# Attention for 64 heads on one core: 18 groups of scores on VectorE instead of 16, and the order of all engines remade

## The chip, the core and the metric

The kernel runs on one core of one Trainium2 chip. A core has several engines that run side by side, each with its own list of instructions in a fixed order: TensorE (PE; its weight loads are listed as PEld) multiplies matrices and writes to PSUM, ScalarE (ACT) computes functions such as exp, VectorE (DVE) and GpSimd (POOL) do elementwise work, SyncE (SP) issues transfers, and 16 DMA engines carry these. An instruction waits on semaphores until what it needs is done; everything behind it on its engine waits with it. The metric is the time of one execution in device microseconds; lower is better.

## The reference

The inputs q, k and v have 8 batches, 8 heads, 512 positions and 64 dimensions each, in float32. The output has the same shape.

```
scores = einsum('bhqd,bhkd->bhqk', q, k) / sqrt(64)
scores = scores - scores.max(axis=-1, keepdims=True)
attn   = exp(scores)
attn   = attn / attn.sum(axis=-1, keepdims=True)
out    = einsum('bhqk,bhkd->bhqd', attn, v)
```

So there are 64 heads with 512 x 512 scores each, 16.8 million exponentials in all.

## The kernel before

**Tiling.** The 64 heads are worked off as 32 pairs (g from 0 to 31, h is 0 or 1). For each pair, q, k and v are loaded by SP (256 KB a transfer, line 509) and cast to fp16 by GpSimd (`cast`, lines 515 and 525). PE transposes q and k (line 558), and VectorE copies the result from PSUM into the tile `tqk` (line 571). PE then computes the scores with keys on the partitions (line 598), in blocks of 128 keys (c from 0 to 3) by 512 queries. Two blocks make a *group*: one PSUM tile `st` of 128 x 1024, of which there are three. There are 128 groups; the last is cut into two halves, so the code counts 129, numbered 0 to 128. Each pair but the first and the last takes four groups in the order c, h; in the last pair the first two groups (124, 125) belong to head 0 and the others to head 1.

**Two ways to an exponential.** Most groups go to ScalarE: one ACTIVATE of exp over 128 x 1024 (line 602) writes the fp16 tile `pt`. The groups listed in `ON_DVE` go to VectorE instead, as six instructions. `raise_` (line 625) reads the scores from PSUM and writes the bits of a power of two with a linear fraction, as a 16-bit integer, into the tile `pd`. That frees the PSUM tile. Then five passes over SBUF, `pass_`: L642 takes the mantissa, L651 the exponent (tile `pe`), L659 squares, L661 is a linear function, and L665 multiplies into `pd`. The exponential of such a group is the sum of `pe` and `pd`, and PE adds both: the product with v has two parts for each block of it instead of one.

**Values.** The weights are not divided before the product with v. The v tile has a column of ones, so that each product (line 704) gives the sum of the weights beside the 64 outputs. A *unit* is 128 queries of one head: four products, one for each c, and one more for each block that VectorE has raised. Seven units share one PSUM tile `o`. When a tile is full, VectorE takes the reciprocal of the sums (L671) and multiplies (L676) into a ring in SBUF, from which SP stores heads (lines 690 and 694). Two PSUM banks serve these tiles and the transposes in turn. The last head, (31, 1), has its own path: `last_values` (line 720), then `finish` (L733, L734) and its own store (L740). The last two other stores are issued by ScalarE.

**What sets the order.** Everything is written out in one list of steps, which the class `Plan` makes while the kernel is built. `Plan.run` steps through a clock of its own, 5 ns at a time, and keeps the time at which each engine comes free. Its methods choose for each engine what it does next: `step_pe` among scores, transposes and values; `step_dve` among copies, raises, reciprocals, multiplies and, when none of these is about to come, passes; `step_pool` and `trigger` place the casts (each waits for a certain VectorE instruction, because the two share access to SBUF in the plan's model); `step_sp` loads and stores. The constants at the head of the class are this model: durations of instructions, waiting times from engine to engine (`TO_ACT`, `TO_DVE`, `TO_PE`, `EXP_DONE`, `PASS_DONE`), rules for what is held back for what (`LATE_*`, `HURRY`, `SOON`, `BACKLOG`, `WAIT`, `SLACK`), and due times for casts (`PAIR`, `DUEK`, `DUEV`, `PRE`). The chip executes the order that comes out, with real waits on semaphores; the plan's clock is not part of the program. `KNOWN` lists groups whose exponential gets one more wait, on a cast six casts back. At most `BITS` = 2 raised groups may be unfinished at a time.

The choice between the engines is made in `scores`:

```
m, grp = self.m, self.groups[self.m]
on_dve = self.for_dve(m)          # m in ON_DVE
if on_dve:
    self.ready.append((t + self.TO_DVE, "raise", (m,)))
```

Of the kernel before, what the change touches and what calls it, by code (L numbers as in the profile page):

```python
# [13 lines left out]
EXP = mybir.ActivationFunctionType.Exp  # L14
# [2 lines left out]

class Plan:

    SLOT, EXP, EXP_DONE, EXP_FIXED = 216, 853, 181, 64  # L20
    INTO, OUT_OF = 96, 96
    TRANSPOSE, V_UNIT = 222, 128
    TO_ACT, TO_DVE, TO_PE = 220, 210, 60

    COPY, NORM, RAISE = (601, 690), (50, 133), (1132, 1215)
    RECIPROCAL = 115
    SCALE, PRODUCT, EXTRA = 333, 600, 29
    COPY_1 = (400, 190)
    NORM_COLUMN, PASS_DONE = 67, 115
    PASSES = (SCALE, SCALE, PRODUCT, SCALE, PRODUCT)  # L30
    BITS = 2
    NEEDS = (None, None, 0, 2, 3)
    FIRST_EXP = 5000
    STEP = 5
    CALM, KEEN = 9000, 4
    FIRST_UNIT = 4
    KNOWN, OVER = (13, 15, 18, 20, 22, 24, 27, 42, 50, 61, 69, 97), 6
    ON_DVE = (5, 10, 16, 25, 28, 39, 44, 54, 63, 66, 74, 81, 91, 96, 103, 116)

    LATE_NORM, LATE_COPY, HURRY, SOON, BACKLOG = 700, 1500, 800, 160, 600  # L40
    LATE_MUL, WAIT = 400, 200
    SLACK, AHEAD = 0, 2

    CAST, CAST_PORT, CAST_DONE, TO_POOL = 557, 475, 130, 150
    SCALE_PORT, PRODUCT_PORT, GAP, REACH = 271, 537, 20, 5
    FIRST_LAND, LOAD, STORE, LATENCY, ISSUE = 5200, 752, 376, 2300, 470
    QUEUED, URGENT = 3500, 16
    PAIRED, STORE_ISSUE = 18, 520
    RAW, QK16, NV, NU = 7, 5, 12, 112
    PAIR, DUEK, DUEV, DUEL, PRE = 3300, 3550, 6000, 5000, 0  # L50

    def __init__(self, groups, pairs, first):
        self.groups, self.pairs = groups, pairs
# [27 lines left out]

        late = {grp[0][0] for m, grp in enumerate(groups) if m in self.ON_DVE}
        due = []
# [121 lines left out]
    def for_dve(self, m):  # L205
        return m in self.ON_DVE

# [126 lines left out]
    def step_dve(self, t):  # L334
# [14 lines left out]
        if now:  # L349
# [15 lines left out]
            if kind == "rec":  # L365
                self.dve = t + self.RECIPROCAL
                self.ready.append((self.dve + self.PASS_DONE, "mul", what))
# [6 lines left out]
            elif kind == "finish":  # L374
                self.dve = t + self.RECIPROCAL + self.PASS_DONE + self.NORM[0] + 4 * self.NORM_COLUMN
            elif kind == "copy":
# [523 lines left out]
```

## Time and profile before

| what | us |
|---|---|
| three runs | 114.32, 114.25, 113.85 |
| median | 114.25 |
| span of the profiled execution, first to last instruction | 112.6 |
| ScalarE busy | 105.7 |
| PE busy | 103.9 |
| VectorE busy | 100.8 |
| GpSimd busy | 66.0 |

The profile gives the span of the execution it recorded, and no other time of it; the runs are timed around the span. Busy time counts overlapping instructions once. Consecutive instructions of VectorE or ScalarE overlap a little, so the price of one in a dense row is the distance from its start to the next start, which is less than its listed duration. L12 stands for line 12 of the kernel. A bracket [0.87 <-PE o L704] says how long the engine was idle before an instruction and what released it. The granted clock of TensorE is 0.999 of full speed over the span.

### The profile page before, as it was taken

The numbers are of one execution on the slowest core, as the hardware profiler recorded it, in microseconds if no ns is written. First come the engines' busy times: TensorE is split into PE (matmuls) and PEld (weight loads), VectorE is DVE, ScalarE is ACT, GpSimd is POOL, SyncE is SP. The second block draws the span as 40 slices with busy tenths as digits, with TensorE's granted clock in tenths as the row PEclk, the third lists the DMA queues.
The fourth block names the chain that finished last, engine by engine and source line by source line (L and its number), as shares of the span: only waits on it lengthen the run. The fifth ranks groups of instructions, "written<-read, shape, count | busy, mean of one in ns | idle before, by whom it ended". The sixth has DMA issues, their size and how long they took to land.

```text
span 112.6 us, 4414 instructions
## 1 busy us (share of the span) xinstructions
PE 103.9 (92%) x1731; PEld 69.8 (62%) x1731; DVE 100.8 (90%) x227; ACT 105.7 (94%) x118; POOL 66.0 (59%) x127
## 2 busy tenths in 40 slices
PE   7987979999799998999989999899999999999980
PEld 7744545766376675748656767577567577675660
DVE  1547999999999999999999999999999999998390
ACT  4688999999999999999999999999999999999970
POOL 2136778639854886496495786876784855600000
PEclk9999999999999999999999999999999999999999
DMA  3999999999999999999999999999998984143344
GB/s 97 269 319 359 346 349 349 354 336 348 348 348 347 350 332 342 348 357 349 372 363 381 353 350 377 345 377 370 332 368 285 357 286 144 53 142 99 121 139 163
DMA packets 35093, 33.84 MB, mean 301 GB/s; under 512 B 2304, under 2 KB 35072, under 8 KB 35072
## 3 DMA queue, kind: packets, MB, share of 16 engines
q1 hardware_dynamic: 34496, 33.04, 90.0%
q10 hardware_dynamic: 576, 0.52, 1.4%
q8 instruction: 13, 0.21, 0.9%
q14 instruction: 8, 0.07, 0.2%
HBM read 25.17 MB, written 8.39 MB: 298 GB/s over the span
## 4 chain that ended last, share of the span: by engine, by line
DMA 36%; PE 24%; DVE 14%; POOL 12%; issue 8%; SPq 2%; ACT 2%; POOLq 0%; ACTq 0%
DMA q<-in_q_dram 21%; PE o L704 12%; DMA out_dram<-ring 9%; PE st L598 8%; POOL qkp L525 8%; DMA v<-in_v_dram 6%; POOL vp L515 3%; DVE pd L625 3%; DVE ring L676 3%; PE tp L558 2%; DVE tqk L571 2%; ACT pt L602 2%; SPq L509 2%; DVE pd L665 1%; DVE m L659 1%
## 5 line engine op out<-in xcount | busy, mean ns | idle before, releaser
L602 ACT ACTIVATE pt<-st 128x1024 f16<-128x1024 f32 (+1 forms) x110 | 100.2, 1136 | 0.4 <-PE st L598 0.4
L704 PEld LDWEIGHTS <-pt 128*128 128x128 f16 x880 | 38.8, 98 | 12.1 <-issue 10.2
L704 PE MATMUL o<-vp,pt 128*128 128x65 f16 x880 | 45.3, 194 | 0.4 <-POOL vp L515 0.3
L598 PE MATMUL st<-tqk 64*128 64x512 f16 (+1 forms) x250 | 41.7, 380 | 2.6 <-ACT pt L602 1.3
L525 POOL CAST qkp<-k 128x512 f16<-128x512 f32 x31 | 22.2, 717 | 11.7 <-DVE rc L671 5.0
L525 POOL CAST qkp<-q 128x512 f16<-128x512 f32 x30 | 21.8, 725 | 9.0 <-DVE rc L671 5.3
L515 POOL CAST vp<-v 128x512 f16<-128x512 f32 x32 | 21.4, 679 | 9.2 <-PE st L598 3.6
L676 DVE TENSOR_TENSOR ring<-o,rc 128x448 f32<-128x448 f32 (+2 forms) x37 | 22.2, 602 | 0.4
L704 PE MATMUL o<-vp,pe 128*128 128x65 f16 x128 | 21.8, 194 | 0.0
L704 PE MATMUL o<-vp,pd 128*128 128x65 f16 x128 | 21.7, 192 | 0.0
L558 PE MATMUL tp<-ident,qkp 128*128 128x128 f16 x248 | 19.6, 220 | 1.4 <-DVE tqk L571 0.8
L558 PEld LDWEIGHTS <-qkp 128*128 128x128 f16 x248 | 14.4, 97 | 9.8 <-issue 4.9
L571 DVE COPY tqk<-tp 128x1024 f16<-128x1024 f16 x30 | 20.2, 680 | 0.0
L625 DVE TENSOR_SCALAR pd<-st 128x1024 uint16<-128x1024 f32 x16 | 19.4, 1214 | 0.7 <-PE st L598 0.7
L598 PEld LDWEIGHTS <-tqk 64*128 64x128 f16 x250 | 10.6, 93 | 11.7 <-issue 4.6
L704 PEld LDWEIGHTS <-pe 128*128 128x128 f16 x128 | 12.5, 98 | 3.5 <-issue 3.4
L704 PEld LDWEIGHTS <-pd 128*128 128x128 f16 x128 | 12.5, 98 | 0.0
L665 DVE TENSOR_TENSOR pd<-pd,m 128x1024 f16<-128x1024 f16 x16 | 10.9, 682 | 0.0
L659 DVE TENSOR_TENSOR m<-m 128x1024 f16<-128x1024 f16 x16 | 10.9, 680 | 0.0
L671 DVE RECIPROCAL rc<-o 128x7 f32<-128x7 f32 (+2 forms) x37 | 7.2, 195 | 2.5 <-PE o L704 2.4
L661 DVE TENSOR_SCALAR m<-m 128x1024 f16<-128x1024 f16 x16 | 6.7, 416 | 0.1
L651 DVE TENSOR_SCALAR pe<-pd 128x1024 uint16<-128x1024 uint16 x16 | 6.5, 407 | 0.0
(52 smaller groups left out, 36.8 us busy)
## 6 DMA issues: line engine op xcount, KB each, us to landing
v<-in_v_dram SPq DMA_DIRECT2D x32, 256.0 KB, 5.9
k<-in_k_dram SPq DMA_DIRECT2D x31, 256.0 KB, 5.9
q<-in_q_dram SPq DMA_DIRECT2D x31, 256.0 KB, 5.9
out_dram<-ring SPq DMA_DIRECT2D x18, 256.0 KB, 5.4
out_dram<-ring SPq DMA_DIRECT2D x25, 128.0 KB, 2.9
k<-in_k_dram ACTq DMA_DIRECT2D x2, 128.0 KB, 2.7
q<-in_q_dram SPq DMA_DIRECT2D x2, 128.0 KB, 2.5
out_dram<-ring ACTq DMA_DIRECT2D x2, 128.0 KB, 1.9
```

The lines of the kernel that those rows point to most:

```text
L515: return nc.gpsimd.tensor_copy(out=vps[g % NV][:, :, :, 0:D], in_=raw[g]["v"][:, :, :, :])
L525: return nc.gpsimd.tensor_copy(out=dst, in_=src[:, :, :, :])
L558: reads[g] = nc.tensor.transpose(tps[g][:, n, i, :], qkp[g][:, n, i, :], ident)
L571: nc.vector.tensor_copy(out=tqk[g][:, :, :], in_=tps.pop(g).rearrange("p n i c -> p n (i c)"))
L598: nc.tensor.matmul(st[:, x, cols], kc, qc[:, cols], start=True, stop=True)
L602: ins = nc.scalar.activation(out=pt[:, :, cols], in_=st[:, :, cols], func=EXP, scale=scale, bias=SHIFT)
L625: nc.vector.tensor_scalar(out=r["pd"][:, :, :], in0=r["st"][:, :, :], scalar1=BITS, scalar2=BIAS, op0=AluOp.mult, op1=AluOp.add,)
L659: ins = nc.vector.tensor_tensor(out=m16, in0=m16, in1=m16, op=AluOp.mult)
L665: ins = nc.vector.tensor_tensor(out=u16, in0=u16, in1=m16, op=AluOp.mult)
L671: dve(nc.vector.reciprocal(out=rcs[u][:, 0:n], in_=o[:, x : x + n, D : D + 1]))
L676: nc.vector.tensor_tensor(out=ring[:, u % NU : u % NU + n, :], in0=o[:, x : x + n, 0:D], in1=rcs.pop(u)[:, 0:n].broadcast_to([P, n, D]), o ...
L704: nc.tensor.matmul(os[u // 7][:, u % 7, :], part[:, y * P : (y + 1) * P], vps[g % NV][:, h, c, :], start=(n == 0), stop=(n == len(parts) - 1),
```

## The change

The two kernels differ only in constants of `Plan`; all functions are the same, and their line numbers too. `ON_DVE` gets two more entries, 120 and 124, and nine of the sixteen others move by one to three. The waiting times and priorities of the model change, so that the plan comes out with another order on every engine.

```
-    SLOT, EXP, EXP_DONE, EXP_FIXED = 216, 853, 181, 64
-    INTO, OUT_OF = 96, 96
+    SLOT, EXP, EXP_DONE, EXP_FIXED = 216, 853, 201, 56
+    INTO, OUT_OF = 92, 88
-    TO_ACT, TO_DVE, TO_PE = 220, 210, 60
+    TO_ACT, TO_DVE, TO_PE = 260, 230, 60
-    RECIPROCAL = 115
+    RECIPROCAL = 125
-    NORM_COLUMN, PASS_DONE = 67, 115
+    NORM_COLUMN, PASS_DONE = 67, 125
-    CALM, KEEN = 9000, 4
+    CALM, KEEN = 11500, 4
-    ON_DVE = (5, 10, 16, 25, 28, 39, 44, 54, 63, 66, 74, 81, 91, 96, 103, 116)
+    ON_DVE = (5, 10, 15, 25, 29, 37, 46, 52, 63, 67, 75, 81, 88, 96, 101, 116, 120, 124)
-    LATE_NORM, LATE_COPY, HURRY, SOON, BACKLOG = 700, 1500, 800, 160, 600
-    LATE_MUL, WAIT = 400, 200
-    SLACK, AHEAD = 0, 2
-    CAST, CAST_PORT, CAST_DONE, TO_POOL = 557, 475, 130, 150
+    LATE_NORM, LATE_COPY, HURRY, SOON, BACKLOG = 1100, 600, 800, 260, 400
+    LATE_MUL, WAIT = 1350, 100
+    SLACK, AHEAD = 400, 2
+    CAST, CAST_PORT, CAST_DONE, TO_POOL = 565, 475, 130, 150
-    PAIR, DUEK, DUEV, DUEL, PRE = 3300, 3550, 6000, 5000, 0
+    PAIR, DUEK, DUEV, DUEL, PRE = 3350, 3300, 5900, 5000, 400
```

In the program that is built, ScalarE's list has two exponentials less, VectorE's 241 rows instead of 229 and PE's 3496 instead of 3464 (weight loads and products counted apart). GpSimd's list has the same length, and the same bytes are loaded and stored.

## The prediction

> **What bounds the kernel now.** I read the engine totals first, then busy time by stage, then VectorE's and ScalarE's instructions in order of time, and last the order of the changed program on each engine. Columns of the totals: busy us, share of the span, instructions.
>
> ```profile
> span 112.6 us, 4414 instructions
> PE 103.9 (92%) x1731; PEld 69.8 (62%) x1731; DVE 100.8 (90%) x227; ACT 105.7 (94%) x118; POOL 66.0 (59%) x127
> ...
> DVE  1547999999999999999999999999999999998390
> ACT  4688999999999999999999999999999999999970
> ```
>
> ScalarE is the busiest, but VectorE's digits are full too, from the fifth slice until the last four. A share over the whole span hides where VectorE's free tenth lies, so the span is cut at three instants of VectorE: 9.98 (its first raise, the first pass over scores), 98.20 (its last raise, group 116) and 110.04 (its work done). The columns are length, then busy time (and instructions) of PE, weight loads, DVE, ACT, POOL.
>
> ```profile
> 9.98:98.20 88.22, 84.81 (x1432) 56.78 (x1430) 87.83 (x181) 88.22 (x97) 62.06 (x117) 1.00 1.02 334
> 98.20:110.04 11.84, 10.86 (x208) 7.39 (x207) 9.12 (x22) 10.78 (x13) 0.56 (x1) 1.00 0.39 127
> ```
>
> For 88 us both engines are full: ScalarE idles 0.00, VectorE 0.39. After 98.20 VectorE idles 11.84 - 9.12 = 2.72. All its free time between its first raise and its end is therefore 3.11 us. PE has 3.4 us free in the first stretch, GpSimd 26: neither is the bound.
>
> ScalarE's exponentials run as one block:
>
> ```profile
> 9.77 99.21 ACT L602 ACTIVATE pt<-st 128x1024 f16<-128x1024 f32 x109 [0.39 <-PE st L598]
> ```
>
> That is 107 full and 2 half instructions, so 99.21 / 108 = 0.919 us each, start to start. The end of the kernel, on VectorE and in the chain that ended last:
>
> ```profile
> 97.43 0.20 DVE L671 RECIPROCAL rc<-o 128x7 f32<-128x7 f32 x1
> 97.66 0.62 DVE L676 TENSOR_TENSOR ring<-o,rc 128x448 f32<-128x448 f32 x1
> 98.20 1.21 DVE L625 TENSOR_SCALAR pd<-st 128x1024 uint16<-128x1024 f32 x1
> 99.33 0.68 DVE L571 COPY tqk<-tp 128x1024 f16<-128x1024 f16 x1
> 99.93 0.42 DVE L642 TENSOR_SCALAR m<-pd 128x1024 uint16<-128x1024 uint16 x1
> 100.26 0.42 DVE L651 TENSOR_SCALAR pe<-pd 128x1024 uint16<-128x1024 uint16 x1
> 100.60 0.69 DVE L659 TENSOR_TENSOR m<-m 128x1024 f16<-128x1024 f16 x1
> 101.20 0.20 DVE L671 RECIPROCAL rc<-o 128x7 f32<-128x7 f32 x1
> 101.32 0.43 DVE L661 TENSOR_SCALAR m<-m 128x1024 f16<-128x1024 f16 x1
> 101.66 0.62 DVE L676 TENSOR_TENSOR ring<-o,rc 128x448 f32<-128x448 f32 x1
> 102.19 0.19 DVE L671 RECIPROCAL rc<-o 128x7 f32<-128x7 f32 x1
> 102.42 0.62 DVE L676 TENSOR_TENSOR ring<-o,rc 128x448 f32<-128x448 f32 x1
> 102.96 0.68 DVE L665 TENSOR_TENSOR pd<-pd,m 128x1024 f16<-128x1024 f16 x1
> 104.51 0.21 DVE L671 RECIPROCAL rc<-o 128x7 f32<-128x7 f32 x1 [0.87 <-PE o L704]
> ...
> 106.86 0.20 DVE L671 RECIPROCAL rc<-o 128x7 f32<-128x7 f32 x1 [1.48 <-PE o L704]
> ...
> 108.69 0.18 DVE L671 RECIPROCAL rc<-o 128x4 f32<-128x4 f32 x1
> 108.91 0.42 DVE L676 TENSOR_TENSOR ring<-o,rc 128x256 f32<-128x256 f32 x1
> 109.37 0.18 DVE L733 RECIPROCAL rc_last<-o_last 128x4 f32<-128x4 f32 x1
> 109.59 0.42 DVE L734 TENSOR_TENSOR obl<-o_last,rc_last 128x256 f32<-128x256 f32 x1
> ```
>
> Until the product of L665 ends at 103.64, VectorE has no gap. From there it only divides finished heads, and waits for PE, which waits for ScalarE. So today ScalarE's last exponentials set the end, with VectorE 5 us ahead of them. From the end of the last instruction (110.01) to the end of the span pass 2.6 us: the last store.
>
> **The change, priced.** *Two exponentials leave ScalarE* (groups 120 and 124; L602 from 108 full instructions to 106): 2 x 0.919 = 1.84 us less there. This is worth something only while ScalarE sets the end.
>
> *Two groups come to VectorE.* VectorE's listing grows from 229 rows to 241, twelve rows, six for each group. Prices are start to start, from the rows above: raise 99.33 - 98.20 = 1.13; L642 0.33; L651 0.34; L659 0.60; L661 0.34; L665 0.60, the distance that L659, of the same shape, has. Together 3.34 us a group, 6.68 for two. The free time is 3.11, so at least 6.68 - 3.11 = 3.57 us cannot be hidden anywhere.
>
> A rule speaks for a higher price. The Trainium skill, VectorE: DVE Perf Modes, section The DRAIN you can't avoid, says that the next op starts only when the pipe of the one before has emptied, and points to an exception for ops that are not held. Priced so, by whole durations (1.21 + 0.42 + 0.42 + 0.69 + 0.43 + 0.68 = 3.85), the two groups would cost 7.70 and the forecast be about 1 us higher. The rows disagree with the plain rule: the copy starts at 99.33, while the raise lasts to 99.41.
>
> *The others of ON_DVE only move* (16 to 15, 28 to 29, 39 to 37, 44 to 46 and so on). In both kernels fifteen raised groups lie ahead of group 116, so ScalarE has as many exponentials ahead of it, and group 116's scores should be ready at the same time. In the trace they are the last of this row, ready at 97.81:
>
> ```profile
> 97.21 0.60 PE L598 MATMUL st<-tqk 64*128 64x512 f16 x4
> ```
>
> The raise of 116 can start about 98.1, 0.1 before now. It cannot start much earlier: its bank of scores is freed by the exponential of group 113, and ScalarE has no gap to give.
>
> *The order is remade.* Ahead of that raise VectorE now has 28 reciprocal-and-multiply pairs instead of 31, so three pairs (0.12 + 0.53 = 0.65 each) move behind it, 1.95 us. Ahead of it this opens as much idle time, which buys nothing, since the raise waits for its scores. The 29 copies and 15 groups of passes ahead of it are the same.
>
> *The end, added up.* Behind the raise of 116 VectorE has three groups (10.02), one copy (0.60), eight full pairs (5.20), the finish (L733, L734: 0.18 + 0.42 = 0.60) and a short pair (109.33 - 108.69 = 0.64): 17.06 us. In the new order the product of group 124 comes ahead of the last full pair and the short one, so it ends 17.06 - 0.65 - 0.64 = 15.77 after the start, if nothing waits: 98.1 + 15.77 = 113.9. Only then PE can do the last 23 of the 24 products of head (31, 0):
>
> ```profile
> 102.33 0.81 PE L704 MATMUL o<-vp,pt 128*128 128x65 f16 x20
> ```
>
> By this row's 0.81 for 20, they take 0.9; with 0.15 for two hand-overs (an estimate: the last rows above show 0.04 between dependent instructions of one engine, 109.33 to 109.37, and two engines should need more) and the short pair, 113.9 + 0.9 + 0.15 + 0.64 = 115.6. The last full pair fits beside PE. The last store has the same 128 KB, and costs the same 2.6: span 118.2, that is 5.6 longer. Raises 120 and 124 fit their scores: ScalarE, one exponential each 0.92, is at group 121 when VectorE reaches raise 120 (98.1 + 1.13 + 0.60 + 0.33 + 0.34 + 0.60 = 101.1). ScalarE ends near 107 and then stands still for 8 us.
>
> *PE* gets 8 more products of L704 per group, 16 in all (a part pe and a part pd in place of one pt). At 0.81 / 20 that is 0.65 us, beside 3.4 us free; in the tail PE waits for VectorE. If that cover were gone it would add 0.65.
>
> *Casts, loads, stores.* All are as many as before. The line CALM now leaves casts up to 11.5 us of the plan's clock free of a VectorE releaser; three loads of v trade places with neighbours; stores move by a few places on SP, and ScalarE's two last stores wait for the last pairs, with ScalarE idle there. GpSimd has 26 us free in the long stretch. I take zero; the bound is given with the third case below. The manual waits of KNOWN stay where they were while the order around them moves: more exponentials carry a wait on ScalarE's own counter, 80 instead of 63. The rows show no price for it (0.919 is with 63 of them); a wait on work 24 instructions old should be free.
>
> The trace lists a span of 112.6 and no other time of that execution; the median of the three runs is 114.25, 1.65 more. Carrying 5.6 over: 119.85.
>
> **The rivals.** (1) *VectorE's tail sets the end*, as added up: 119.8. What speaks for it: 87.83 of 88.22, and the new order itself, which puts six tiles of values (beside the last head's) behind the last scores, where there was one. Against: nothing that I see in the rows.
>
> (2) *VectorE uses all its free time*: the raise of 116 comes early, or work is moved into the gap. It gives the floor, 3.57: 117.8. Against: the scores of 116 hang on ScalarE.
>
> (3) *The remade order also starves ScalarE or VectorE ahead of the tail.* For pairs 7 to 9 the transposes now lie 3, 1 and 2 groups of scores ahead of use, instead of 4, 2 and 4. A late pair costs up to a copy behind a raise (0.60 + 1.13 = 1.73) less one exponential of cover, 0.8 us. One to three such stalls, each handed on to the tail: 120.6 to 122.3. Against: ScalarE's idle 0.00 in the long stretch, with leads of 2 in it.
>
> (4) *Faster: ScalarE still sets the end.* Then the time falls by 1.84, to 112.4. This decides if the product of 124 ends by ScalarE's last exponential, about 107, instead of 113.9: VectorE would need 7 us more room at the end than its rows give. By the Trainium skill, Perfetto Trace Analysis, section Identifying the Most-Contended Engine, the engine with the highest occupancy is to be relieved first. By that rule 94% against 90% would favour this change, and this is the outcome it gives. The stretch with both engines full, above, is why I do not follow it.
>
> That the change does nothing is out: the twelve rows are there.
>
> **How the numbers follow.** Chances: (1) 0.63, (2) 0.10, (3) 0.21, (4) 0.02, something else 0.04. The forecast is (1), 119.8. The range reaches from just under (2) to just over (3): 117.5 to 122.6; it leaves out (4) and the rest. Within 0.5% (0.57 us, about what runs that spread from 113.85 to 114.32 can tell from no change) I put 0.01, for a mixture of (2) and (4). Slower: 0.97.
>
> **What will show it.** Right: ScalarE's block of L602 ends near 107, with 106 full instructions; VectorE's raise of 116 starts at 97.8 to 98.6 with an idle stretch of 1 to 2 us ahead of it; from there VectorE is full for some 16 us, and the last row before the short pair is L665 near 114; the chain that ended last runs through VectorE in the last 15 us. Wrong: gaps in ScalarE's block ahead of 98 (case 3); a raise of 116 well ahead of 97 (case 2); distances between VectorE's starts in the tail other than 0.33, 0.60 and 1.13 (a price); a last L665 ahead of ScalarE's end (case 4).

## The result

The changed kernel takes 119.32 us (median of four runs, 118.98 to 119.67); the kernel before took 114.05 us beside it. The ratio is 1.0478, with a 95% interval of 1.0451 to 1.0505: 5.3 us slower. The profiled execution has a span of 117.6 us and took 119.42.

The totals of the changed kernel, and VectorE's and ScalarE's busy tenths in 40 slices:

```profile
span 117.6 us, 4458 instructions
PE 106.2 (90%) x1747; PEld 71.0 (60%) x1747; DVE 107.2 (91%) x239; ACT 103.9 (88%) x116; POOL 64.1 (55%) x127
...
DVE  1557999999999999999999999999999969999991
ACT  4699999999999999999999999999999999993000
```

ScalarE has 1.8 us less to do, VectorE 6.4 us more. ScalarE now falls silent three slices before the end, and VectorE works through to it. The stretches, cut as before: from VectorE's first raise (9.44) to its raise of group 116 (97.57), from there to the end of its work (115.04), and the last part of that, from L733 on. Columns: length, then busy time of PE, weight loads, DVE, ACT, POOL.

```profile
9.44:97.57 88.13, 82.99 (x1333) 54.23 (x1332) 86.47 (x175) 88.05 (x97) 60.58 (x116) 1.00 1.01 329
97.57:115.04 17.47, 15.49 (x325) 11.37 (x322) 17.02 (x40) 9.42 (x12) 0.11 (x1) 1.00 0.37 123
107.58:115.04 7.46, 5.48 (x152) 4.88 (x148) 7.14 (x19) 0.00 (x0) 0.00 (x0) 1.00 0.54 178
```

The long stretch has its old length (88.13 for 88.22). All of the loss lies behind the raise of 116: 17.47 us where there were 11.84, with VectorE idle for 0.45 of them. (The raise itself comes 0.63 earlier, so VectorE's work ends 5.0 us later: 115.04 for 110.01.) ScalarE's block, and the rows of VectorE that the prediction named:

```profile
8.36 98.64 ACT L602 ACTIVATE pt<-st 128x1024 f16<-128x1024 f32 x108
```

```profile
94.76 0.21 DVE L671 RECIPROCAL rc<-o 128x7 f32<-128x7 f32 x1 [0.39 <-PE o L704]
...
96.79 0.20 DVE L671 RECIPROCAL rc<-o 128x7 f32<-128x7 f32 x1 [0.57 <-PE o L704]
97.03 0.62 DVE L676 TENSOR_TENSOR ring<-o,rc 128x448 f32<-128x448 f32 x1
97.57 1.21 DVE L625 TENSOR_SCALAR pd<-st 128x1024 uint16<-128x1024 f32 x1
98.70 0.68 DVE L571 COPY tqk<-tp 128x1024 f16<-128x1024 f16 x1
...
107.24 0.20 DVE L671 RECIPROCAL rc<-o 128x7 f32<-128x7 f32 x1
107.58 0.18 DVE L733 RECIPROCAL rc_last<-o_last 128x4 f32<-128x4 f32 x1
107.79 0.42 DVE L734 TENSOR_TENSOR obl<-o_last,rc_last 128x256 f32<-128x256 f32 x1
...
112.73 0.68 DVE L665 TENSOR_TENSOR pd<-pd,m 128x1024 f16<-128x1024 f16 x1
113.33 0.20 DVE L671 RECIPROCAL rc<-o 128x7 f32<-128x7 f32 x1
...
114.40 0.18 DVE L671 RECIPROCAL rc<-o 128x4 f32<-128x4 f32 x1 [0.21 <-PE o L704]
114.62 0.42 DVE L676 TENSOR_TENSOR ring<-o,rc 128x256 f32<-128x256 f32 x1
```

ScalarE ends at 8.36 + 98.64 = 107.00. VectorE ends 8.04 us later; before it was 110.01 - 108.98 = 1.03, where 108.98 is ScalarE's end (9.77 + 99.21). The chain that ended last shows what meets at L733, 0.6 us behind ScalarE's end (columns: start, us, what):

```profile
105.92 1.13 PE o L704 x32
107.04 0.51 PE o_last L720 x16
107.55 0.02 issue
107.58 0.20 DVE rc_last L733
...
113.47 0.91 PE o L704 x23
```

At 107.5 two lines arrive together. VectorE has finished L671 at 107.44 and PE the last head's products at 107.55. That coincidence is what the experiments are about: which of the two would have set the end alone?

### The profile page after: what moved, and what is told of

It is laid out like the page before. It is cut to its first block, busy times and chain, and to the rows that moved or that the text cites. A ratio compares the mean times of both kernels' runs of the same rounds, so it can differ in the third digit from the quotient of the medians.

```text
span 117.6 us, 4458 instructions
## 1 busy us (share of the span) xinstructions
PE 106.2 (90%) x1747; PEld 71.0 (60%) x1747; DVE 107.2 (91%) x239; ACT 103.9 (88%) x116; POOL 64.1 (55%) x127
## 4 chain that ended last, share of the span: by engine, by line
ACT 37%; PE 36%; DVE 18%; issue 7%; ACTq 0%
ACT pt L602 36%; PE o L704 14%; PE st L598 12%; DVE pd L625 4%; PE tp L558 4%; DVE ring L676 3%; PE st_0a L751 3%; DVE tqk L571 3%; DVE m L659 2%; DVE pd L665 2%; DVE m L642 1%; DVE rc L671 1%; ACT pt L801 1%; DVE pe L651 1%; PE st L794 1%
## 5 line engine op out<-in xcount | busy, mean ns | idle before, releaser
L602 ACT ACTIVATE pt<-st 128x1024 f16<-128x1024 f32 (+1 forms) x108 | 98.6, 1142 | 0.1
L704 PE MATMUL o<-vp,pt 128*128 128x65 f16 x864 | 47.2, 194 | 1.3 <-DVE ring L676 0.5
L704 PE MATMUL o<-vp,pe 128*128 128x65 f16 x144 | 24.4, 195 | 0.6 <-DVE ring L676 0.4
L704 PE MATMUL o<-vp,pd 128*128 128x65 f16 x144 | 24.0, 192 | 0.4 <-DVE pd L665 0.4
L525 POOL CAST qkp<-q 128x512 f16<-128x512 f32 x30 | 20.4, 680 | 7.2 <-PE st L598 2.1
L625 DVE TENSOR_SCALAR pd<-st 128x1024 uint16<-128x1024 f32 x18 | 21.9, 1218 | 0.8 <-PE st L598 0.7
L676 DVE TENSOR_TENSOR ring<-o,rc 128x448 f32<-128x448 f32 (+2 forms) x37 | 22.3, 605 | 0.2
L704 PEld LDWEIGHTS <-pe 128*128 128x128 f16 x144 | 13.9, 98 | 3.2 <-issue 2.4
L704 PEld LDWEIGHTS <-pd 128*128 128x128 f16 x144 | 14.0, 98 | 0.5 <-DVE pd L665 0.5
L665 DVE TENSOR_TENSOR pd<-pd,m 128x1024 f16<-128x1024 f16 x18 | 12.2, 680 | 0.0
L671 DVE RECIPROCAL rc<-o 128x7 f32<-128x7 f32 (+2 forms) x37 | 7.4, 200 | 1.5 <-PE o L704 1.2
L642 DVE TENSOR_SCALAR m<-pd 128x1024 uint16<-128x1024 uint16 x18 | 7.8, 432 | 0.0
```

The costliest lines, as they stand in the source:

```text
L525: return nc.gpsimd.tensor_copy(out=dst, in_=src[:, :, :, :])
L602: ins = nc.scalar.activation(out=pt[:, :, cols], in_=st[:, :, cols], func=EXP, scale=scale, bias=SHIFT)
L625: nc.vector.tensor_scalar(out=r["pd"][:, :, :], in0=r["st"][:, :, :], scalar1=BITS, scalar2=BIAS, op0=AluOp.mult, op1=AluOp.add,)
L642: ins = nc.vector.tensor_scalar(out=r["m"][:, :, :], in0=u[:, :, :], scalar1=0x03FF, scalar2=0x3C00, op0=AluOp.bitwise_and, op1=AluOp.bitw ...
L665: ins = nc.vector.tensor_tensor(out=u16, in0=u16, in1=m16, op=AluOp.mult)
L676: nc.vector.tensor_tensor(out=ring[:, u % NU : u % NU + n, :], in0=o[:, x : x + n, 0:D], in1=rcs.pop(u)[:, 0:n].broadcast_to([P, n, D]), o ...
```

## The experiments

Theory A is that of the prediction: VectorE's work behind the raise of 116 sets the end. Rival B: the remade order costs the time, not the two groups. Later C (PE's values set the end) and D (both stand close behind each other) are added. Ratios are to the kernel before in the same set of runs (113.9 to 114.0 us).

**1. The two groups taken out, all other constants new.**

```
-    ON_DVE = (5, 10, 15, 25, 29, 37, 46, 52, 63, 67, 75, 81, 88, 96, 101, 116, 120, 124)
+    ON_DVE = (5, 10, 15, 25, 29, 37, 46, 52, 63, 67, 75, 81, 88, 96, 101, 116)
```

> The changed kernel with 120 and 124 taken out of ON_DVE again; all other constants stay new, and the plan makes its order from them. Theory A (VectorE's work behind the raise of group 116 sets the end): two groups of 3.34 us leave VectorE, ScalarE gets 1.84 us back, and the time returns to about that of the kernel before, 113.5 to 115.0. Rival B (the remade order costs the time, whatever the number of groups): it stays above 117.5. If both share it, it lands between, and the share of the two groups is the difference to 119.3.

Measured: 116.82 us, ratio 1.0262 (1.0213 to 1.0311). It lies between the two expectations: the remade order alone costs 2.85 us, and the two groups on top of it 2.5. ScalarE's block in this run, and the end of the chain:

```profile
7.88 100.43 ACT L602 ACTIVATE pt<-st 128x1024 f16<-128x1024 f32 x110
```

```profile
106.47 0.38 PE st L598 x2
106.84 2.13 PE o L704 x64
108.98 0.12 PE o_last L720 x4
109.10 0.91 PE o L704 x28
110.01 0.02 issue
110.03 0.22 DVE rc L671
```

ScalarE ends at 108.31, no later than in the kernel before. Behind the last scores PE works off 96 products in a row, 3.2 us, before VectorE's row at 110.03, and 28 more follow. In this order 25 units of values (beside the last head's) lie behind the last scores; in the kernel before it was 4. The new constants push values back, and PE pays for it at the end, when nothing else is left to do beside them.

**2. The two groups alone, on the old order's constants.**

```
-    ON_DVE = (5, 10, 16, 25, 28, 39, 44, 54, 63, 66, 74, 81, 91, 96, 103, 116)
+    ON_DVE = (5, 10, 16, 25, 28, 39, 44, 54, 63, 66, 74, 81, 91, 96, 103, 116, 120, 124)
```

> The kernel before with 120 and 124 added to its own ON_DVE and nothing else changed. Theory A: VectorE has 3.1 us free and gets 6.7 us, so at least 3.6 us more than 114.05, that is 117.6 to 119.5. Rival B: the old constants make a good order, so it stays below 115.5.

Measured: 119.68 us, ratio 1.0493 (1.0445 to 1.0541). That is 0.2 above theory A's range. With every other constant at its old value (the plan still makes its order anew) the two groups cost 5.7 us, so theory A's part holds without the new constants. But 2.85 and 5.7 are not added up in the changed kernel, which loses 5.3. Two causes share one end.

**3. The new constants with the old list of 16 groups.**

```
-    ON_DVE = (5, 10, 15, 25, 29, 37, 46, 52, 63, 67, 75, 81, 88, 96, 101, 116, 120, 124)
+    ON_DVE = (5, 10, 16, 25, 28, 39, 44, 54, 63, 66, 74, 81, 91, 96, 103, 116)
```

> The changed kernel with the old ON_DVE of 16 groups: the new waiting times and priorities alone. Theory A: no work is added, so 113.5 to 115.0, and any distance from 114.05 is the price of the remade order. Rival B: above 117.5.

Measured: 117.23 us, ratio 1.0300 (1.0255 to 1.0345), like the first run. So the nine groups that move by one to three make no difference that can be told; the waiting times and priorities do.

**4. Less work for VectorE, in the changed kernel's own order.**

```
     def pass_(m, s):
         r = raised[m]
+        if m in (120, 124) and s in (2, 3):
+            return
```

> The changed kernel in its own order, with L659 and L661 of groups 120 and 124 left out (four instructions of VectorE; the exponentials of these two groups come out without their cubic correction, so this part of the computation is missing). Theory A: each left-out pair frees 0.60 + 0.34 us on VectorE ahead of the last product, so 1.88 us less, 117.4 (117.2 to 117.9). Rival C (PE's six tiles of values behind the last scores set the end, and VectorE only follows): 119.0 to 119.5, no change.

Measured: 119.00 us, ratio 1.0463 (1.0414 to 1.0512), at most 0.3 less and within the scatter. Theory A expected 1.88 less: it falls, as far as it says that VectorE alone sets the end. The rows show where the freed time went (the same instructions have lines higher by two here, L735 is L733):

```profile
105.94 0.20 DVE L673 RECIPROCAL rc<-o 128x7 f32<-128x7 f32 x1 [0.46 <-PE o L706]
...
107.33 0.18 DVE L735 RECIPROCAL rc_last<-o_last 128x4 f32<-128x4 f32 x1 [0.29 <-PE o_last L722]
...
111.42 0.21 DVE L673 RECIPROCAL rc<-o 128x7 f32<-128x7 f32 x1 [0.44 <-PE o L706]
```

VectorE, now quicker, stands waiting for PE at three places, 1.19 us together. Half of the cut lies ahead of L733 (group 120) and half behind it (group 124). From the raise of 116 (at 97.32 in this run) to L733 it is 10.01 us, as in the changed kernel, so the first half gained nothing.

**5. The same cut in the old order with 18 groups.** The edit of run 4 on the kernel of run 2.

> The kernel before with 120 and 124 added, in that order, with L659 and L661 of groups 120 and 124 left out (their exponentials come out without the cubic correction). In this order VectorE was full from the raise of 116 at 97.53 to 112.39, with one wait of 1.5 us behind it. Theory A (VectorE's work alone sets the end): 1.88 us less than 119.68, that is 117.8 (117.5 to 118.3). Theory D (PE's products stand right behind VectorE's work in every such tail): 119.0 or more, as in the new order, where the same cut gave 0.3.

Measured: 118.43 us, ratio 1.0405 (1.0363 to 1.0447), 1.25 less than run 2. It lies between the expectations, 0.1 us above A's range. Here VectorE's work counts for about half (0.88 us between VectorE's ends in the two traces) to two thirds (1.25 by the medians); part of the rest is again lost in front of the last head:

```profile
106.98 0.18 DVE L735 RECIPROCAL rc_last<-o_last 128x4 f32<-128x4 f32 x1 [0.67 <-PE o_last L722]
```

**6. LATE_MUL alone, on the kernel before.**

```
-    LATE_MUL, WAIT = 400, 200
+    LATE_MUL, WAIT = 1350, 200
```

> The kernel before with one constant changed, LATE_MUL from 400 to 1350: a pass may then be put ahead of a multiply that has long been ready. 16 groups, the old list. In the order this leaves 18 units of values behind the last scores instead of 4, beside the last head. Theory D (values pushed back behind the last exponentials lengthen the tail by PE's time for them): 14 units of 4 to 5 products at 0.035 us are 2.0 to 2.5 us, so 116.0 to 116.6. Theory A (only VectorE's work counts, and none is added): 113.7 to 114.5.

Measured: 116.53 us, ratio 1.0230 (1.0201 to 1.0259), inside D's range. One priority, with no work added, costs 2.5 us. The reading is this: a multiply (L676) frees the PSUM bank of its tile; if passes go ahead of it, PE's values start later, and more of them are left for the end. The count of units in the order (18 for 4) and the size of the loss fit it; no row of this run was used to show it.

**7. Fewer products for PE.**

```
+        light = [b for m in (88, 96, 101, 116, 120, 124) for b in groups[m]]
-        parts = [(c, part) for c in range(NI) for part in blocks[(g, c, h)]]
+        parts = [(c, part) for c in range(NI)
+                 for part in blocks[(g, c, h)][1 if (g, c, h) in light else 0 :]]
```

> The changed kernel in its own order, with the 48 products of the part pe of groups 88, 96, 101, 116, 120 and 124 left out (this part of those heads' sums is missing); VectorE does all it did. PE has 48 x 0.035 = 1.7 us less to do. Theory A: VectorE sets the end, 119.0 to 119.5, no change. Theory C (PE alone sets it): 117.3 to 117.8. Theory D (both stand close behind each other): small, up to 0.6 less.

Measured: 119.09 us, ratio 1.0458 (1.0430 to 1.0485), 0.2 less. Theory C falls: PE alone does not set the end either.

**8. Both cuts together.** The edits of runs 4 and 7 in one kernel.

> The cuts of the two single runs together: L659 and L661 of groups 120 and 124, and the 48 products of the part pe (both parts are missing from the output). Theory D (two chains of nearly equal length, VectorE's and PE's): the two cuts together give more than their sum, 1.2 to 2.0 us less than 119.3, so 117.3 to 118.1. Theory A or C: no more than the single cut that works.

Measured: 118.61 us, ratio 1.0417 (1.0385 to 1.0448), 0.7 less. The intervals do not tell that from the single cuts together (0.5), and it is well short of D's 1.2 to 2.0. So something else holds the end as well. What is left is ScalarE, whose last exponentials the last head's products need. This run's rows (L740 is L733 here):

```profile
7.67 98.76 ACT L602 ACTIVATE pt<-st 128x1024 f16<-128x1024 f32 x108
```

```profile
106.94 0.18 DVE L740 RECIPROCAL rc_last<-o_last 128x4 f32<-128x4 f32 x1 [0.29 <-PE o_last L727]
```

With VectorE and PE both relieved, L733 still starts 0.51 us behind ScalarE's end (7.67 + 98.76 = 106.43).

**9. More work for ScalarE near its end.**

```
+        if m in (125, 126):
+            nc.scalar.activation(
+                out=pt[:, :, cols], in_=st[:, :, cols], func=EXP, scale=scale, bias=SHIFT
+            )
```

> The changed kernel with the exponentials of groups 125 and 126 done twice on ScalarE (same result written twice): 2 x 0.92 = 1.84 us more on ScalarE, near the end, where it stands still for 8 us afterwards. As the prediction put it (VectorE's tail sets the end, ScalarE has time to spare there): 119.2 to 119.6, no change. Theory D, as it now stands (VectorE's L733 of the last head waits in line for ScalarE's last exponentials and PE's products behind them, and had waited only 0.14 us there): the whole tail behind L733 moves with it, 1.5 to 1.84 us more, 120.8 to 121.2.

Measured: 121.11 us, ratio 1.0601 (1.0539 to 1.0664), 1.8 us more than the changed kernel by the medians, 1.4 by the ratios. The engine that stands still for the last 8 us passes on nearly all of its delay. ScalarE's last two rows are a pair, and VectorE waits for what depends on it (L737 is L733 here):

```profile
107.78 1.08 ACT L602 ACTIVATE pt<-st 128x512 f16<-128x512 f32 x2
```

```profile
107.56 0.19 DVE L675 RECIPROCAL rc<-o 128x7 f32<-128x7 f32 x1
109.25 0.18 DVE L737 RECIPROCAL rc_last<-o_last 128x4 f32<-128x4 f32 x1 [1.50 <-PE o_last L724]
```

ScalarE ends at 108.86 instead of 107.00, and VectorE stands 1.50 us before L733. Everything queued behind L733, among it all five passes of group 124 and five pairs of reciprocal and multiply, moves back with it. It needs nothing from the last head; it only stands behind it in VectorE's list.

The traces now answer the question asked above. Each line gives ScalarE's end, the time from there to the start of L733, and the time from there to VectorE's end (us, worked out from rows like those shown):

| kernel | ScalarE's end | to L733 | L733 to VectorE's end |
|---|---|---|---|
| before | 108.98 | 0.39 | 0.64 |
| changed | 107.00 | 0.58 | 7.46 |
| run 2 (old constants, 18 groups) | 106.78 | 0.39 | 7.40 |
| run 4 (less for VectorE) | 106.74 | 0.59 | 7.17 |
| run 5 (run 2, less for VectorE) | 106.59 | 0.39 | 6.71 |
| run 7 (less for PE) | 106.96 | 0.52 | 7.26 |
| run 8 (less for both) | 106.43 | 0.51 | 6.76 |
| run 9 (more for ScalarE) | 108.86 | 0.39 | 7.47 |

L733 follows ScalarE's end by 0.39 to 0.59 us in all of them, whichever engine has less to do, and moves with it in run 9. In the changed kernel PE's products arrive last there, by the chain shown; but 0.39 behind ScalarE's end is the earliest start seen, so VectorE and PE together add at most 0.2 to what ScalarE's line allows. What runs 4, 7 and 8 gain lies behind L733: 0.29, 0.20 and 0.70 us, in a stretch where VectorE and PE wait for each other by turns. Of the 5.03 us by which VectorE ends later than in the kernel before (115.04 for 110.01), ScalarE's earlier end gives back 1.98, the step to L733 adds 0.19, and the work behind L733 adds 6.82.

**10. The new constants, 16 groups, LATE_MUL at its old value.**

```
-    LATE_MUL, WAIT = 1350, 100
+    LATE_MUL, WAIT = 400, 100
```

> The changed kernel with 120 and 124 taken out and LATE_MUL back at 400; all other constants new. The order has 9 units of values behind the last scores instead of 25. If what the new constants cost comes from these units (4 to 5 products at 0.035 us each): 16 x 0.15 = 2.4 us less than 116.82, 114.2 to 115.0. If the backlog is only a mark of something else in the order: 116.2 or more.

Measured: 115.70 us, ratio 1.0135 (1.0084 to 1.0186): 1.1 less than run 1, neither the 2.4 expected nor nothing. The rows split it:

```profile
8.28 22.30 ACT L602 ACTIVATE pt<-st 128x1024 f16<-128x1024 f32 x24
30.79 57.07 ACT L602 ACTIVATE pt<-st 128x1024 f16<-128x1024 f32 x62 [0.21 <-PE st L598]
88.14 21.31 ACT L602 ACTIVATE pt<-st 128x1024 f16<-128x1024 f32 x24 [0.29 <-PE st L598]
```

```profile
110.63 0.17 DVE L733 RECIPROCAL rc_last<-o_last 128x4 f32<-128x4 f32 x1
110.83 0.42 DVE L734 TENSOR_TENSOR obl<-o_last,rc_last 128x256 f32<-128x256 f32 x1
```

From ScalarE's end (88.14 + 21.31 = 109.45) to VectorE's end (111.25) it is 1.8 us, where run 1 has about 3.6. That is the shorter backlog. But ScalarE's own end comes 1.14 later: its block starts 0.40 later, and two gaps of 0.21 and 0.29 are seen in it, each released by PE's scores. That PE does values there instead of scores is likely, but not shown; which constant opens these gaps was not tried.

**11 and 12. Two lists of 15 groups, with other priorities.** Both were chosen with the plan's own clock; the waiting times are the changed kernel's. The lines that replace its own, first of run 11, then of run 12:

```
+    ON_DVE = (5, 14, 24, 31, 34, 45, 52, 57, 66, 72, 82, 87, 99, 104, 110)
+    LATE_NORM, LATE_COPY, HURRY, SOON, BACKLOG = 12700, 17400, 800, 2100, 200
+    LATE_MUL, WAIT = 23950, 6050
+    SLACK, AHEAD = 200, 2
+    PAIR, DUEK, DUEV, DUEL, PRE = 3625, 3200, 13800, 3000, 4400
```

```
+    ON_DVE = (5, 10, 17, 27, 32, 38, 46, 54, 61, 67, 76, 82, 92, 98, 120)
+    LATE_NORM, LATE_COPY, HURRY, SOON, BACKLOG = 1650, 8550, 800, 0, 4100
+    LATE_MUL, WAIT = 4200, 50
+    SLACK, AHEAD = 0, 2
+    PAIR, DUEK, DUEV, DUEL, PRE = 2850, 1500, 4800, 7000, 200
```

> A list of 15 groups, the last of them 110, with the changed kernel's waiting times and other priorities (passes ahead of everything that is not a copy or a raise); 4 units behind the last scores. ScalarE gets one exponential more than in the kernel before. Theory: where ScalarE sets the end and nothing is behind it, the time is that of before plus at most 0.92, less what the tail gains by VectorE being done earlier: 113.6 to 115.0. It beats 114.05 only if VectorE's early end saves more than 0.92.

> Another list of 15 groups, its last one 120, so a raise near the end, but only one; the changed kernel's waiting times; 4 units behind the last scores. Theory: one late group is 3.34 us of VectorE in a tail that has 2.7 us free, and ScalarE has one exponential more: 113.8 to 115.2. If a raise as late as 120 is by itself what costs the time, 116 or more.

Measured: 115.29 us (ratio 1.0124, 1.0044 to 1.0203; 0.3 us above the range given) and 114.91 us (1.0096, 1.0062 to 1.0129; inside it). Neither beats the kernel before. Run 12 at its end, ScalarE first:

```profile
108.69 0.78 ACT L602 ACTIVATE pt<-st 128x512 f16<-128x512 f32 x1
```

```profile
110.08 0.42 DVE L734 TENSOR_TENSOR obl<-o_last,rc_last 128x256 f32<-128x256 f32 x1
```

110.50 - 109.47 = 1.03 us behind ScalarE's end, exactly as in the kernel before: with nothing else queued there, the end is ScalarE's end plus a fixed piece. A raise as late as 120 leaves no tail of its own here, and neither does LATE_MUL at 4200. That points to how much is left behind the last scores (4 units here) as what counts, and not to the value of the constant; these runs change many constants at once and do not part them.

## Why the prediction was right

**The number.** 119.8 was forecast, 119.32 measured. Case (1) put the loss into the work behind the raise of 116, and that is where it lies; its reason, that VectorE alone sets the end, is only half right (below). By its own steps:

- *The raise of 116*: 98.1 forecast, 97.57 measured, just outside the 97.8 to 98.6 given. ScalarE's block now runs from 8.36 without the pause that the kernel before had ahead of 9.77, so all scores come a little earlier. Run 2 has no such pause either, with VectorE's rows up to 30 us in the same order as in the kernel before, so it need not come from the change. This is nearly the whole error of the sum (a span of 118.2 forecast, 117.6 measured).
- *The idle time ahead of it*: 1 to 2 us forecast; 88.13 - 86.47 = 1.66 over the whole long stretch, with 0.39 and 0.57 of it in the two rows shown, just ahead of the raise.
- *The work behind it*: 15.77 us to the end of the last product's slot, if nothing waits. The short reckoning from rows of the kernel before came out at 113.33 - 97.57 = 15.76.
- *PE's last 23 products*: 0.9 forecast, 0.91 in the chain. *The two hand-overs* around them: 0.15 estimated; the chain has gaps of 0.05 and 0.02 there. (The rows that the estimate names, 109.33 to 109.37, are not dependent on each other.) *The store*: 2.6 forecast; 117.6 - 115.04 = 2.56.
- *The prices* of a raised group: 98.70 - 97.57 = 1.13 for the raise, as before. The whole-duration prices, which the forecast had weighed and left, would have put the raise 0.08 too high here.
- *The floor* of 3.57 us for two more groups on a full VectorE: both kernels with 18 groups and all their work lie above it, at 5.3 and 5.7.
- *ScalarE's end near 107*: 107.00.
- *The chain that ended last* was to run through VectorE for the last 15 us. It does so only from L733 at 107.58; ahead of that it runs through PE's scores and products. This sign failed.

**What the sum hid.** Two sentences of it were wrong although the number was right. The first: ScalarE "then stands still for 8 us", which the sum treats as time to spare. Run 9 gave it 1.84 us of work, and VectorE's end moved by 1.68 (115.04 to 116.72). The finish of the last head (L733, L734) is in the middle of VectorE's list, and it needs ScalarE's last exponentials. The second: "in the tail PE waits for VectorE". Up to 107.58 PE was busy without a break (15.49 - 5.48 = 10.01 us of the 10.01 from 97.57); it waits only behind that. Runs 4, 7 and 8 show the consequence. Taking 1.88 us from VectorE gave 0.3, taking 1.7 us from PE gave 0.2, both together 0.7. The listed work of VectorE was the right sum because three lines (VectorE's, PE's, ScalarE's) met within about 0.6 us at L733, not because VectorE was alone. To that extent the sum came out right by luck.

**What the remade order cost.** The prediction priced it as three pairs moved behind the raise, 1.95 us, and saw six tiles of values behind the last scores, but named the two groups as the cause. Run 1 says that the order alone costs 2.85 us, and run 6 that one priority is enough for 2.5. Run 2 says that the two groups alone cost 5.7. The two groups suffice for the whole loss and the order for about half of it, so undoing one is not enough. That PE's backlog is the mechanism of the order's cost rests on run 6's agreement, on run 1's chain and on the shorter tail of run 10; it is argued from these, not isolated. Why the new constants with 16 groups and the old LATE_MUL still lose 1.5 us is settled only in part: ScalarE's gaps are seen, their cause is not.

**The rivals.** Case (2), the floor, did not come: the scores of 116 end at 97.29 and the raise starts at 97.57, so it could not have come much earlier. Case (3), starved engines ahead of the tail: there is no gap in ScalarE's block, and the long stretch has its old length. Case (4), where the engine with the highest share of busy time is relieved and the time falls by 1.84: ScalarE's end did come 1.98 earlier (108.98 to 107.00), and the end of the kernel 5 us later.

## What to carry to other kernels

Where two engines are both full, work moved from the busier to the other can only be hidden as far as it fits into the other's idle time; count that idle time by stage, in us, and not as a share of the span. At the end of a kernel, add up what stands in each engine's list *behind* the last instruction of the engine that paces everything: this sum is the tail. Look at the order in the list too: what stands behind a waiting instruction waits with it, as in run 9. An engine that is idle for long may still have set the end, if something in the middle of another engine's list waits for it; give it more work in an experiment before calling its time free.

## What the runs showed of the hardware

TensorE's granted clock fell by half in the tail of run 2, and the last products took 60% longer. The stretches from 107 us on, in that run (the eighth number is the granted clock):

```profile
107.00:109.00 2.00, 0.17 (x5) 0.04 (x2) 1.90 (x6) 0.00 (x0) 0.00 (x0) 1.00 0.54 183
109.00:111.00 2.00, 1.40 (x39) 1.28 (x39) 2.00 (x7) 0.00 (x0) 0.00 (x0) 1.00 0.04 14
111.00:112.44 1.44, 0.24 (x1) 0.10 (x1) 1.35 (x4) 0.00 (x0) 0.00 (x0) 0.53 0.31 103
112.44:113.93 1.49, 1.45 (x23) 1.29 (x23) 0.00 (x1) 0.00 (x0) 0.00 (x0) 0.50 0.77 252
```

The 23 products take 1.46 us at a clock of 0.50, where the changed kernel, at 1.00, takes 0.91 for the same. This is 0.55 us of run 2's tail; run 2 is 0.4 us slower than the changed kernel. The drop came at about 111 us, after 4 us in which PE was busy for 1.57. The Trainium skill, TensorE: Matmul & The Clock Gate, section What's actually happening, says that the clock goes to half after about one window of 3.4 us in which the array is idle. The run agrees on the half; it shows the drop with PE 40% busy and no gap longer than about 2 us, so a partly filled stretch can be enough. Run 5, the same order with less for VectorE, shows the same drop: a clock of 0.50 from 110.50 on, after 3.5 us (107.00 to 110.50) in which PE was busy for 1.46, with a longest gap of 1.64. In the changed kernel PE had 5.48 us of work in the last 7.46 and kept its clock.
